# One array for the first tiles, norms by token, an earlier compression and moved tile sizes in a two-layer hybrid decoder

## The chip, the cores and the metric

The kernel runs on one core of one Trainium2 chip. The metric is the device time of the whole program in microseconds (us), from three runs: 1609.97, 1611.32 and 1611.22, median 1611.22. TensorE (PE) does the matmuls, ScalarE (ACT) and VectorE (DVE) convert and post-process, GpSimd (POOL) multiplies some tiles, and SyncE (SP) issues most of the DMAs.

## The reference

Two layers work on x of 256 tokens by 2048 features in float32. Each layer does

```python
h = rmsnorm(x, norm_w)
proj = einsum("bsd,dp->bsp", h, w_in)
(q, kc, vc, ks, vs, kw, vw, gate, z_attn, xbc, dt, z_ssm) = split_columns(proj)
k_cmp = rope(compress_blocks(kc, pe_k, w1_k, w2_k), pos_cmp)
v_cmp = compress_blocks(vc, pe_v, w1_v, w2_v)
y_attn = rmsnorm(nsa_attention(...) * silu(z_attn), norm_attn_w)
y_ssm = grouped_rmsnorm((ssd(silu(conv(xbc)), dt) + d_skip * xs) * silu(z_ssm), norm_ssm_w)
x = x + einsum("bsm,md->bsd", concat([y_attn, y_ssm]), w_out)
```

and a last rmsnorm with `final_norm_w` follows the second layer. The compression turns overlapping blocks of 32 keys (and values) into 15 compressed ones through two small matrices w1 and w2; the attention has a compressed, a selected and a windowed branch.

## The kernel before

Weights come as tiles of 128 x 1024 float32 (512 KB). SP loads them in the order of use into five raw buffers `wr` (`pump_dma`, line 147); a load is issued when DVE has used up the oldest one. Float32 accuracy is had from two reduced-precision parts: ACT copies the tile to `wh` (high part, line 122) and DVE subtracts it, `wl` = `wr` - `wh` (line 125). Both are issued by `split` (line 154), two tiles ahead of PE. The same is done to h: a tile `h` holds the high and the low part of 256 tokens each.

The work is a list (`items`, line 55). A projection item takes half of the 16 k-tiles of one tile of 128 output columns: 16 matmuls, eight of 512 moving columns with `wh` and eight of 256 with `wl`. One such item is called a slot. The first four column tiles (NF) do all their first halves (slots 0 to 3), then all their second halves (slots 4 to 7); later ones do the two halves in turn. The accumulators of later column tiles share two buffers, "pj". After the column tiles come the output projection's items in two halves ("o", 64 slots).

Post-processing is written as generators that are listed in `sides` and are moved on one step per slot by `tick` (line 327); WAITS counts the slots that each step waits. The evacuation of a finished column tile is put into `pending` and is done by `flush` in the following slot, ahead of that slot's `split`.

Around the change:

- **The head.** `FIRST` (line 92): weight 0 comes in three pieces on ACT's queue. x^T comes by `load_x` (line 185) on SP's queue, in five pieces between the first weight tiles, then `par` and `con` (lines 202, 203). Position numbers come on POOL's queue (line 384). Six matmuls on a zero tile stand before slot 0 (line 365) and eight more inside it (`WARM`, line 964).
- **The norm of layer 1** is applied to the projection's results, by a tile `rr` that holds one factor per token. ACT squares x^T in four pieces of 1024 columns, DVE adds them up in five steps (`first_slots`, line 389), PE sums over partitions with four matmuls (`rms`, line 280) at slot 5, ACT and DVE take the root at slots 6 and 7. Layer 2 has sums of squares by token from the end of layer 1 (`part`) and uses `spread_norm` (line 309) at slots 0, 1 and 2: small steps by token, then two matmuls that spread the factor over the partitions. x by token (`xT`) is loaded in slots 20 to 26 of layer 1.
- **The compression.** W1S, W1N, W1B = 9, 2, 4 (line 34): counted from the first kc tile, a group of four w-items (16 small matmuls) is put behind slot 9 and every second one after it, eight groups in all. Their moving operands are written by `build_U` (line 594) on DVE, from the evacuated kc and vc tiles. `cmp_side` (line 605) then makes the compressed keys KT and values VC, and the first `att_side` (line 688) starts when all groups are issued and the keys are there. `v_side` (line 659) transposes value tiles on PE (line 665) into a PSUM tile "t" of two buffers and copies them out on ACT and DVE as V. `gd_side` waits for rr and makes the gates.
- **The last phase.** In the second half of the output projection, `add` (line 991) adds a finished tile of 128 x 512 to `xT`, squares it on ACT and, in the last layer, multiplies it by `final_norm_w` on POOL (line 998) for the first three of four column blocks. `out_norm` (line 906) scales the rows: columns 0 to 1023 on ACT, 1024 to 1535 on DVE, the rest with the weight on DVE; all stores are issued by SP in this order.

Of the kernel before, what the change touches and what calls it, by code (L numbers as in the profile page):

```python
# [33 lines left out]
W1S, W1N, W1B = 9, 2, 4  # L34
# [53 lines left out]
def body(ctx: ExitStack, tc: tile.TileContext, wst, w1, xin, xtk, pos, w2, par, con, fin, y):  # L88
    nc = tc.nc
    ACT, DVE, PE, POOL = nc.scalar, nc.vector, nc.tensor, nc.gpsimd  # L90
    RS, RA = 5, 1
    FIRST = ((0, 256), (256, 512), (512, 1024))
# [81 lines left out]
    sqr = xt.rearrange("p a b -> p (a b)")  # L174
# [10 lines left out]
    def load_x(a, b):  # L185
        c = NK + SEQ * a if a else 0
        nc.sync.dma_start(xw[:, c:NK + SEQ * b], xin[:, c:NK + SEQ * b])

    raw[0] = sb([128, 1024], "wr", bufs=NR)
# [12 lines left out]
    nc.sync.dma_start(prm, par[0])  # L202
    nc.sync.dma_start(cst, con)
    pump_dma()
# [88 lines left out]
    part = sb([128, 2, 4], "part")  # L293

    def norm(tb, r):
        b = sb([128, 4], "nrm", bufs=2)
# [12 lines left out]
    def spread_norm(dst):  # L309
        r = sb([128, 2], "rt2")  # L310
        gens = [norm(tb, r[:, tb:tb + 1]) for tb in range(2)]
        for g in gens:
            next(g)
        for g in gens:
            for _ in g:
                pass
        yield
        ps = pst("b2", (128, 1024))
        for tb in range(2):
            mm(ps[:, 128 * tb:128 * tb + 128], r[:, tb:tb + 1].to_broadcast([128, 128]), ident, True, True)  # L320
        yield
        act(dst, ps[:, 0:256])
# [42 lines left out]
    for _ in range(6):  # L365
        mm(pz, wz[:, 0:128], wz, True, True)
# [3 lines left out]
    def make_h(a, b):  # L370
        for k in range(a, b):
            h[k] = sb([128, 512], f"h{k}", F32R)
            scaled(attn[:, k], nw0[:, k:k + 1], h[k])
# [4 lines left out]
    for j, (a, b) in enumerate(FIRST):  # L378
        make_h((0, 1, 2)[j], (1, 2, 4)[j])
        act(hi_t[0][:, a:b], raw[0][:, a:b])  # L380
        lo(lo_t[0][:, a:b], raw[0][:, a:b], hi_t[0][:, a:b])
# [4 lines left out]
    def square(c):  # L386
        act(sqr[:, c:c + 1024], reg[:, c:c + 1024], AF.Square)

    def first_slots(slot):
        if slot < 2:  # L390
            make_h(8 + 4 * slot, 12 + 4 * slot)
            square(1024 * slot)
        elif slot == 2:
            square(2048)
            tt(sqr[:, 0:1024], sqr[:, 0:1024], sqr[:, 1024:2048], OP.add)
        elif slot == 3:
            square(3072)
            tt(sqr[:, 0:1024], sqr[:, 0:1024], sqr[:, 2048:3072], OP.add)
        elif slot == 4:
            tt(sqr[:, 0:1024], sqr[:, 0:1024], sqr[:, 3072:4096], OP.add)  # L400
            tt(sqr[:, 0:512], sqr[:, 0:512], sqr[:, 512:1024], OP.add)

    sqs = [sqr[:, 0:256], sqr[:, 256:512]]

    for L in range(DEPTH):
# [500 lines left out]
        def out_norm(tb):  # L906
            r = sb([128, 1], f"rt{tb}")
            g = norm(tb, r)
            for _ in g:
                pass  # L910
            for c in range(4):
                a = xt[:, tb, 512 * c:512 * c + 512]
                if c == 3:
                    stt(a, a, r, fnw[:, 512 * c:512 * c + 512], OP.mult, OP.mult)
                elif c == 2:
                    DVE.tensor_scalar(a, a, r, None, op0=OP.mult)
                else:
                    act(a, a, scale=r)
                if c in (1, 2, 3):
                    b = 0 if c == 1 else 512 * c  # L920
                    nc.sync.dma_start(y[:, tb, b:512 * c + 512], xt[:, tb, b:512 * c + 512])
# [8 lines left out]
        for it in ITEMS:  # L930
# [21 lines left out]
            if it[0] == "p":  # L952
# [6 lines left out]
                for a in range(0, 8, n):  # L959
                    for k in range(a, a + n):  # L960
                        mm(ps, wh[:, k], src[k], first and k == 0, False)
                    for k in range(a, a + n):
                        mm(ps[:, 0:256], wl[:, k], src[k][:, 0:256], False, last and k == 7)
                    if L == 0 and slot == 0:
                        for _ in range(WARM[a]):
                            mm(pz, wz[:, 0:128], wz, True, True)
                flush()
                split(i)
            else:
# [52 lines left out]

                last4 = L + 1 == DEPTH and half and cb == 3 and kp > 3
# [13 lines left out]
                else:  # L1037
# [6 lines left out]
                    if kp == 7:  # L1044
                        add(1)
                        if half and L + 1 < DEPTH:
                            sides.append(turn())
# [13 lines left out]
            if slot == (0 if L else RS):  # L1061
                next(rgen)
            if slot == (1 if L else RS + RA):
                next(rgen)
            if slot == (2 if L else RS + RA + 1):
                for _ in rgen:
                    pass
                rr.append(rt_)
# [80 lines left out]

def layout(x, positions, norm_w, w_in, cmp_pe_k, cmp_w1_k, cmp_w2_k, cmp_pe_v, cmp_w1_v, cmp_w2_v,  # L1150
           conv_w, conv_b, dt_bias, a_log, d_skip, norm_attn_w, norm_ssm_w, w_out, final_norm_w):
    A = lambda v: np.asarray(v)
    return [
        pack_weights(A(w_in), A(w_out)),
        pack_w1(A(cmp_w1_k), A(cmp_w1_v)),
        np.ascontiguousarray(np.concatenate([
            cols(A(norm_w)[0]), A(x)[0].T.reshape(NK, 128, SEQ).transpose(1, 0, 2).reshape(128, NK * SEQ)], 1)),
# [26 lines left out]
```

## Time and profile before

| what | value |
|---|---|
| time, median of three runs | 1611.22 us |
| time of the profiled execution | 1612.35 us |
| its span | 1610.6 us |
| PE busy | 1582.5 us (98%), 9042 matmuls |
| weight loads of PE | 1353.0 us (84%), beside the matmuls |
| DVE busy | 1219.2 us (76%) |
| ACT busy | 1056.3 us (66%) |
| POOL busy | 383.9 us (24%) |
| HBM read | 298.20 MB, 186 GB/s over the span |

Busy times are those of one profiled execution, on an axis that starts with its span. A busy PE is not PE at its peak: the granted clock of a stretch is a second number to be read beside it, as tenths or hundredths of 2.4 GHz. A line such as L125 is that of a helper, so tiles say more than lines. The waits name the instruction that released the engine last.

### The profile page before, as it was taken

To read this page: it belongs to the slowest core of one execution; us is meant where nothing else is said; L and a number is where in the kernel's file an instruction comes from. 1 tells how busy PE (TensorE), PEld (TensorE's weight loads), DVE (VectorE), ACT (ScalarE), POOL (GpSimd) and SP (SyncE) were. 2 spreads that over 40 slices of the span, in tenths; PEclk is the share of its full clock that TensorE was granted. 3 is DMA by queue.
4 is the path that set the end of the run, shared out by engine and by line. 5 is a ranking of instruction groups with operands and counts; after the bars stand their busy time and mean duration, and the time that the engine had idled before them with its cause. 6 is when DMAs were issued, how large, how long until landed. Compare 5 with 4: busy or idle time off the path is not lost.

```text
span 1610.6 us, 24881 instructions
## 1 busy us (share of the span) xinstructions
PE 1582.5 (98%) x9042; PEld 1353.0 (84%) x9042; DVE 1219.2 (76%) x2113; ACT 1056.3 (66%) x1918; POOL 383.9 (24%) x314
## 2 busy tenths in 40 slices
PE   8999999999899999999999999999998999999997
PEld 7888888878788888888888888888787888888876
DVE  6888988887688786674578888888867878766654
ACT  6587777754687787544456777777447778865443
POOL 1233433431123231100012333333301323210010
PEclk9999999999999999999999999999999999999999
DMA  7575566677444444565646666666863454455653
GB/s 267 187 253 189 191 205 209 206 248 256 130 157 134 156 151 153 195 192 166 207 158 197 201 206 192 190 200 222 273 224 121 142 158 145 157 169 171 235 177 110
DMA packets 101994, 301.98 MB, mean 188 GB/s; under 512 B 9952, under 2 KB 26912, under 8 KB 101744
## 3 DMA queue, kind: packets, MB, share of 16 engines
q1 hardware_dynamic: 101024, 297.99, 56.4%
q0 software_dynamic: 416, 1.88, 0.4%
q8 instruction: 71, 1.16, 0.3%
q10 hardware_dynamic: 432, 0.52, 0.1%
q14 instruction: 51, 0.42, 0.1%
HBM read 298.20 MB, written 2.16 MB: 186 GB/s over the span
## 4 chain that ended last, share of the span: by engine, by line
PE 93%; DVE 2%; ACT 2%; DMA 1%; issue 1%; POOL 0%; ACTq 0%; SPq 0%; DVEq 0%; POOLq 0%
PE ppj L137 77%; PE po L137 7%; PE pb L137 6%; DVE wl L125 1%; ACT wh L122 1%; PE pt L137 1%; DMA wr<-wst 1%; PE pt L523 0%; PE pt L766 0%; PE po L773 0%; PE pt L767 0%; DMA V<-w 0%; DVE xT L125 0%; ACT A L122 0%; DVE A L128 0%
## 5 line engine op out<-in xcount | busy, mean ns | idle before, releaser
L125 DVE TENSOR_TENSOR wl<-wr,wh 128x1024 fp32r<-128x1024 f32 (+1 forms) x502 | 642.6, 1285 | 218.4 <-ACT wh L122 217.5
L122 ACT ACTIVATE wh<-wr 128x1024 fp32r<-128x1024 f32 (+1 forms) x502 | 517.8, 1048 | 85.6 <-PE ppj L137 46.2
L137 PE MATMUL ppj<-h,wh 128*128 128x512 f32 x1456 | 464.6, 400 | 3.1 <-DVE h L128 3.1
L137 PE MATMUL ppj<-s,wh 128*128 128x512 f32 x1456 | 462.7, 399 | 0.0
L137 PEld LDWEIGHTS ppj<-h,wl 128*128 128x128 f32 x1456 | 274.9, 189 | 65.1
L137 PEld LDWEIGHTS ppj<-s,wl 128*128 128x128 f32 x1456 | 274.4, 188 | 65.1
L137 PE MATMUL ppj<-h,wl 128*128 128x256 f32 x1456 | 288.3, 279 | 0.0
L137 PE MATMUL ppj<-s,wl 128*128 128x256 f32 x1456 | 287.3, 279 | 0.0
L340 POOL TENSOR_TENSOR uu<-uu,rr 128x256 f32<-128x256 f32 x120 | 147.7, 1232 | 525.3 <-DVE uu L125 524.0
L137 PEld LDWEIGHTS ppj<-h,wh 128*128 128x128 f32 x1456 | 223.4, 190 | 9.5 <-issue 3.3
L137 PEld LDWEIGHTS ppj<-s,wh 128*128 128x128 f32 x1456 | 222.8, 189 | 5.0 <-issue 2.7
L122 ACT ACTIVATE ev<-ppj 128x256 f32<-128x256 f32 x182 | 68.7, 378 | 210.7 <-PE ppj L137 193.7
L137 PE MATMUL ppj<-wh,h 128*128 128x512 f32 x384 | 120.4, 391 | 0.0
L137 PE MATMUL ppj<-wh,s 128*128 128x512 f32 x384 | 120.1, 391 | 0.0
L340 POOL TENSOR_TENSOR za<-za,rr 128x256 f32<-128x256 f32 x34 | 39.6, 1165 | 274.6 <-DVE za L125 239.2
L137 PEld LDWEIGHTS ppj<-wh,h 128*128 128x128 f32 x384 | 72.1, 188 | 15.6 <-DVE xT L125 0.7
L137 PEld LDWEIGHTS ppj<-wh,s 128*128 128x128 f32 x384 | 72.1, 188 | 15.5 <-DVE xT L125 0.7
L125 DVE TENSOR_TENSOR uu<-ppj,ev 128x256 f32<-128x256 f32 x116 | 48.7, 420 | 47.1 <-ACT ev L122 46.9
L122 ACT ACTIVATE A<-A,nm 128x128 f32<-128x128 f32 (+2 forms) x192 | 75.4, 394 | 7.8 <-DVE nm L716 7.6
L137 PE MATMUL ppj<-wl,s 128*128 128x512 f32 x192 | 74.9, 390 | 0.8 <-DVE wl L125 0.8
L137 PE MATMUL ppj<-wl,h 128*128 128x512 f32 x192 | 74.8, 389 | 0.0
L128 DVE SCALAR_TENSOR_TENSOR att<-uu,par,att 128x255 f32<-128x255 f32 (+2 forms) x96 | 60.5, 630 | 2.3
(244 smaller groups left out, 1980.9 us busy)
## 6 DMA issues: line engine op xcount, KB each, us to landing
wr<-wst SPq DMA_DIRECT2D x499, 512.0 KB, 3.5
V<-w SPq DMA_DIRECT2D x64, 256.0 KB, 4.8
B<-cum SPq DMA_DIRECT2D x16, 512.0 KB, 4.6
B<-cum SPq DMA_DIRECT2D x16, 256.0 KB, 5.7
xT<-xtk SPq DMA_DIRECT2D x4, 512.0 KB, 6.8
att<-xin SPq DMA_DIRECT2D x3, 512.0 KB, 8.5
att<-fin POOLq DMA_DIRECT2D x1, 1024.0 KB, 8.9
y<-xT SPq DMA_DIRECT2D x2, 512.0 KB, 2.7
```

The costliest lines, as they stand in the source:

```text
L122: ACT.activation(out, in_, f, **kw)
L125: DVE.tensor_tensor(out, a, b, op=op)
L128: DVE.scalar_tensor_tensor(out, a, s, b, op0=op0, op1=op1)
L137: PE.matmul(out, lhsT, rhs, start=start, stop=stop, skip_group_check=True)
L340: POOL.tensor_tensor(dst, dst, rr[0], op=OP.mult)
```

## The change

1. **Head.** A new array holds x tile k and slice k of weight 0 side by side for the first eight k, after the norm weights (`pack_head`). It comes in four loads on SP's queue (`HEAD`: 205, 393, 590 and 393 KB), and nothing comes on ACT's queue. Weights 1 and 2, x tiles 8 to 11, weight 3, x tiles 12 to 15 (into a tile "B"), weight 4, the first half of x by token (1 MB) and weight 5 follow in this order; weight 6 and the second half of x by token come behind the first `split`. `con` is loaded in slot 0, `par` and the positions in slot 3, all on SP. h of tiles 8 to 15 is made in slots 1 and 2 (before: 0 and 1). `WARM` gives six matmuls inside slot 0 (eight) and five stand before it (six). Weight 1 is converted in two pieces of 512.
2. **Norms.** Layer 1 uses `spread_norm` too, at slots 5, 6 and 7, from two squares of 2048 columns of x by token on ACT in slots 4 and 5. The four squares of x^T, DVE's five adds and the four matmuls of `rms` there go. Layer 2's steps are at slots 1, 3 and 4.
3. **Compression** from slot 8 (`W1S`), so each of its eight groups stands one slot earlier, and with it `cmp_side` and the condition of the first `att_side`.
4. **Order in the first 24 slots:** `split` stands ahead of `flush`.
5. **Last phase.** The multiplication by `final_norm_w` goes from POOL to DVE, two and four slots later (`weigh`). `out_norm` does columns 1024 to 1535 first and stores them, then ACT's half, stored from ACT's queue, then the last quarter.
6. **Sizes.** `con` has 848 columns (835), `part` 8 per token block (4); small tiles rt0, rt1 and rt2 go. Tiles behind `con` then start at multiples of 64 bytes.

```diff
-C_ID, C_MK, C_M2, C_CM, C_RV, C_I4, C_IF, C_SG, NC_ = 0, 128, 512, 768, 800, 801, 833, 834, 835
+C_ID, C_MK, C_M2, C_CM, C_RV, C_I4, C_IF, C_SG, NC_ = 0, 128, 512, 768, 800, 801, 833, 834, 848
-WARM = (1, 2, 1, 1, 1, 1, 1, 0)
+WARM = (2, 1, 0, 1, 1, 0, 1, 0)
-W1S, W1N, W1B = 9, 2, 4
+W1S, W1N, W1B = 8, 2, 4
-    RS, RA = 5, 1
-    FIRST = ((0, 256), (256, 512), (512, 1024))
+    HEAD = ((0, 1), (1, 3), (3, 6), (6, 8))
+    RS = ((5, 6, 7), (1, 3, 4))
...
+    NX = NK + 8 * 384
+    head = xw[:, NK:NX].rearrange("p (k c) -> p k c", k=8)
+    raw0 = head[:, :, 256:384]
+    xb = sb([128, 1536], "B", bufs=2)[:, 0:1024].rearrange("p (k c) -> p k c", k=4)
...
-    for a, b in FIRST:
-        nc.scalar.dma_start(raw[0][:, a:b], wst[0][:, a:b])
-    load_x(0, 1)
-    load_x(1, 4)
-    load_x(4, 8)
+    for a, b in HEAD:
+        c = NK + 384 * a if a else 0
+        nc.sync.dma_start(xw[:, c:NK + 384 * b], xin[:, c:NK + 384 * b])
     pump_one()
     pump_one()
-    load_x(8, 12)
+    nc.sync.dma_start(xw[:, NX:NX + 1024], xin[:, NX:NX + 1024])
     pump_one()
-    load_x(12, 16)
+    nc.sync.dma_start(xb, xin[:, NX + 1024:NX + 2048].rearrange("p (k c) -> p k c", k=4))
     pump_one()
-    nc.sync.dma_start(prm, par[0])
-    nc.sync.dma_start(cst, con)
-    pump_dma()
+    nc.sync.dma_start(xt[:, 0], xtk[:, 0])
+    pump_one()
...
-    for j, (a, b) in enumerate(FIRST):
-        make_h((0, 1, 2)[j], (1, 2, 4)[j])
...
-    make_h(4, 8)
-    split(1 - LH)
-    nc.gpsimd.dma_start(posi, bass.AP(tensor=pos.tensor, offset=pos.offset, ap=[[0, 128], [1, SEQ]]))
+    for a, b in HEAD:
+        make_h(a, b)
+        act(w0h[:, a:b], raw0[:, a:b])
+        lo(w0l[:, a:b], raw0[:, a:b], w0h[:, a:b])
+    split(1 - LH, 512)
+    nc.sync.dma_start(xt[:, 1], xtk[:, 1])
...
     def first_slots(slot):
...
+        if slot == 0:
+            nc.sync.dma_start(cst, con)
         elif slot == 3:
+            nc.sync.dma_start(prm, par[0])
+            nc.sync.dma_start(posi, bass.AP(tensor=pos.tensor, offset=pos.offset, ap=[[0, 128], [1, SEQ]]))
+        elif slot in (1, 2):
+            make_h(4 + 4 * slot, 8 + 4 * slot)
+        elif slot in (4, 5):
+            act(reg[:, 0:DM], xt[:, slot - 4], AF.Square, accum_out=part[:, slot - 4, 3:4])
...
+            q = [xt[:, tb, 512 * c:512 * c + 512] for c in range(4)]
+            DVE.tensor_scalar(q[2], q[2], r, None, op0=OP.mult)
+            nc.sync.dma_start(y[:, tb, 1024:1536], q[2])
+            for c in range(2):
+                act(q[c], q[c], scale=r)
+            nc.scalar.dma_start(y[:, tb, 0:1024], xt[:, tb, 0:1024])
+            stt(q[3], q[3], r, fnw[:, 1536:2048], OP.mult, OP.mult)
+            nc.sync.dma_start(y[:, tb, 1536:2048], q[3])
...
+                if i < 24:
+                    split(i)
                 flush()
                 split(i)
...
-                        if L + 1 == DEPTH and cb < 3:
-                            POOL.tensor_tensor(a, a, fnw[:, 512 * cb:512 * cb + 512], op=OP.mult)
...
+                def weigh(cb=cb):
+                    for tb in range(2):
+                        yield
+                        yield
+                        a = x4[:, tb, cb]
+                        tt(a, a, fnw[:, 512 * cb:512 * cb + 512], OP.mult)
...
-                rgen = spread_norm(rt_) if L else rms(sqs, DM, rt_, sb([128, 256], "uu", bufs=3))
+                rgen = spread_norm(rt_)
...
-                if slot >= 20 and slot < 28 and slot % 2 == 0:
-                    c = (slot - 20) // 2
-                    nc.sync.dma_start(xt[:, :, 512 * c:512 * c + 512], xtk[:, :, 512 * c:512 * c + 512])
...
+            if slot in RS[L]:
+                next(rgen, None)
+                if slot == RS[L][2]:
+                    rr.append(rt_)
...
+def pack_head(norm_w, x, wst):
+    xk = x[0].T.reshape(NK, 128, SEQ).transpose(1, 0, 2)
+    first = np.concatenate([xk[:, 0:8], wst[0].reshape(128, 8, 128)], 2).reshape(128, 8 * 384)
+    return np.ascontiguousarray(np.concatenate([cols(norm_w[0]), first, xk[:, 8:].reshape(128, 2048)], 1))
```

## Rows read from the trace of the kernel before

**Rows 1.** Page, busy time by engine, and the chain's shares by engine

```profile
PE 1582.5 (98%) x9042; PEld 1353.0 (84%) x9042; DVE 1219.2 (76%) x2113; ACT 1056.3 (66%) x1918; POOL 383.9 (24%) x314
...
PE 93%; DVE 2%; ACT 2%; DMA 1%; issue 1%; POOL 0%; ACTq 0%; SPq 0%; DVEq 0%; POOLq 0%
```

**Rows 2.** Waits of PE: tile, line <- releaser: us, times, longest us

```profile
PE pt L665 <- DVE V L125: 8.7, 2, 4.4
PE ppj L137 <- DVE h L128: 3.1, 2, 2.1
PE po L137 <- DVE wl L125: 1.6, 2, 0.8
...
PE pb L137 <- DVE rt L128: 1.1, 2, 0.9
PE pt L137 <- DVE att L128: 1.1, 1, 1.1
```

**Rows 3.** Half-clock windows: us; PE, PEld, DVE, ACT, POOL; PEclk; DMA share; GB/s

```profile
12.01:15.42 3.41, 3.41 (x10) 2.83 (x11) 3.14 (x5) 3.41 (x7) 0.00 (x0) 0.50 1.03 414
422.33:425.02 2.69, 2.69 (x9) 2.30 (x10) 2.32 (x10) 0.34 (x1) 0.00 (x0) 0.50 0.15 20
1215.55:1220.33 4.78, 4.78 (x16) 4.10 (x17) 4.21 (x17) 0.34 (x1) 0.00 (x0) 0.50 0.37 113
```

**Rows 4.** DMA issues, first 40 us: tiles, queue, KB, us to landing

```profile
wr<-wst ACTq DMA_DIRECT2D x1, 256.0 KB, 8.4
```

**Rows 5.** ACT, timeline 0 to 20: start us, us, instruction, idle before

```profile
4.24 0.51 ACT L122 ACTIVATE h<-att 128x256 fp32r<-128x256 f32 x1 [0.81 <-DMA att<-xin]
...
10.08 0.63 ACT L122 ACTIVATE wh<-wr 128x512 fp32r<-128x512 f32 x1 [2.92 <-DMA wr<-wst]
...
15.70 1.04 ACT L122 ACTIVATE xT<-att 128x1024 f32<-128x1024 f32 x1
```

**Rows 6.** Chain of waits, 12 to 22: start us, us, what

```profile
15.79 2.80 PE po L137 x16
```

**Rows 7.** ACT, timeline of the tail

```profile
1602.71 0.29 ACT L122 ACTIVATE nrm<-part,nrm 128x1 f32<-128x1 f32 x1
...
1603.86 1.33 ACT L122 ACTIVATE xT<-xT,rt 128x512 f32<-128x512 f32 x2 [0.61 <-DVE rt L128]
```

**Rows 8.** DVE, timeline 22 to 38

```profile
23.50 1.22 DVE L125 TENSOR_TENSOR wl<-wr,wh 128x1024 fp32r<-128x1024 f32 x1
24.64 1.22 DVE L125 TENSOR_TENSOR xT<-xT 128x1024 f32<-128x1024 f32 x1
...
36.85 0.42 DVE L128 SCALAR_TENSOR_TENSOR rr<-rr,uu 128x256 f32<-128x256 f32 x1
```

**Rows 9.** ACT, timeline around the first wait for V

```profile
414.12 0.38 ACT L122 ACTIVATE ev<-ppj 128x256 f32<-128x256 f32 x1 [5.53 <-PE ppj L137]
...
415.47 1.28 ACT L118 ACT_TABLE_LOAD   x1
...
419.12 2.20 ACT L122 ACTIVATE VC<-pt 32x128 fp32r<-32x128 f32 x8
421.34 0.38 ACT L122 ACTIVATE V<-pt 128x256 fp32r<-128x256 f32 x1
```

**Rows 10.** DVE, timeline 330 to 337

```profile
334.52 1.10 DVE L125 TENSOR_TENSOR B<-uu,par 128x256 f32<-128x256 f32 x2
```

**Rows 11.** PE, timeline 333 to 336

```profile
334.12 0.63 PE L137 MATMUL ppj<-h,wh 128*128 128x512 f32 x2
```

**Rows 12.** DVE, timeline of the last phase

```profile
1579.38 1.47 DVE L125 TENSOR_TENSOR wl<-wr,wh 128x1024 fp32r<-128x1024 f32 x1 [1.74 <-ACT wh L122]
1580.77 0.67 DVE L125 TENSOR_TENSOR xT<-xT,ppj 128x512 f32<-128x512 f32 x1
```

**Rows 13.** POOL, timeline of the last phase

```profile
1578.48 1.29 POOL L998 TENSOR_TENSOR xT<-xT,att 128x512 f32<-128x512 f32 x1 [17.73 <-ACT za L122]
```

**Rows 14.** SP, timeline of the tail

```profile
1605.22 1.63 SPq L921 DMA_DIRECT2D y<-xT  x3
```

More of the change, by code (lines that the diff above doesn't have):

```diff
@@ L183, in pump_one @@
         state["dma"] += 1
[L185 to L189, printed above, removed]
-    state["dma"] = 1
-    for a, b in FIRST:
-        nc.scalar.dma_start(raw[0][:, a:b], wst[0][:, a:b])
-    load_x(0, 1)
-    load_x(1, 4)
-    load_x(4, 8)
+    NX = NK + 8 * 384
+    head = xw[:, NK:NX].rearrange("p (k c) -> p k c", k=8)
+    raw0 = head[:, :, 256:384]
+    xb = sb([128, 1536], "B", bufs=2)[:, 0:1024].rearrange("p (k c) -> p k c", k=4)
+    xk = ([head[:, k, 0:256] for k in range(8)]
+          + [xw[:, NX + SEQ * k:NX + SEQ * k + SEQ] for k in range(4)] + [xb[:, k] for k in range(4)])
+    raw[0] = None
+    state["dma"] = 1
+    for a, b in HEAD:
+        c = NK + 384 * a if a else 0
+        nc.sync.dma_start(xw[:, c:NK + 384 * b], xin[:, c:NK + 384 * b])
     pump_one()
     pump_one()
-    load_x(8, 12)
+    nc.sync.dma_start(xw[:, NX:NX + 1024], xin[:, NX:NX + 1024])
     pump_one()
-    load_x(12, 16)
+    nc.sync.dma_start(xb, xin[:, NX + 1024:NX + 2048].rearrange("p (k c) -> p k c", k=4))
     pump_one()
-    nc.sync.dma_start(prm, par[0])
-    nc.sync.dma_start(cst, con)
-    pump_dma()
+    nc.sync.dma_start(xt[:, 0], xtk[:, 0])
+    pump_one()
     ident = cst[:, C_ID:C_ID + 128]
@@ L291, in rms, with norm @@
         stt(v, v, 1.5, y0, OP.add, OP.mult)
-    part = sb([128, 2, 4], "part")
-    def norm(tb, r):
-        b = sb([128, 4], "nrm", bufs=2)
+    part = sb([128, 2, 8], "part")
+    POOL.memset(part, 0.0)
+    def norm(tb, b):
+        r = b[:, 3:4]
         tt(b[:, 0:1], part[:, tb, 0:1], part[:, tb, 1:2], OP.add)
@@ L309, in spread_norm @@
     def spread_norm(dst):
-        r = sb([128, 2], "rt2")
-        gens = [norm(tb, r[:, tb:tb + 1]) for tb in range(2)]
+        b = [sb([128, 4], "nrm", bufs=2) for _ in range(2)]
+        gens = [norm(tb, b[tb]) for tb in range(2)]
         for g in gens:
@@ L364, in body @@
     pz = pst("b2", (128, 1024))[:, 0:512]
-    for _ in range(6):
+    for _ in range(5):
         mm(pz, wz[:, 0:128], wz, True, True)
@@ L377, in body @@
     lo_t[0] = sb([128, 1024], "wl", F32R, bufs=NL)
-    for j, (a, b) in enumerate(FIRST):
-        make_h((0, 1, 2)[j], (1, 2, 4)[j])
-        act(hi_t[0][:, a:b], raw[0][:, a:b])
-        lo(lo_t[0][:, a:b], raw[0][:, a:b], hi_t[0][:, a:b])
-    make_h(4, 8)
-    split(1 - LH)
-    nc.gpsimd.dma_start(posi, bass.AP(tensor=pos.tensor, offset=pos.offset, ap=[[0, 128], [1, SEQ]]))
-    def square(c):
-        act(sqr[:, c:c + 1024], reg[:, c:c + 1024], AF.Square)
-    def first_slots(slot):
[L390 to L395, printed above, removed]
-        elif slot == 3:
[L397 to L403, printed above, removed]
+    w0h, w0l = (t[0].rearrange("p (k c) -> p k c", k=8) for t in (hi_t, lo_t))
+    for a, b in HEAD:
[4 more added lines that the diff above has]
+    nc.sync.dma_start(xt[:, 1], xtk[:, 1])
+    def first_slots(slot):
+        if slot == 0:
+            nc.sync.dma_start(cst, con)
+        elif slot == 3:
+            nc.sync.dma_start(prm, par[0])
[4 more added lines that the diff above has]
+            act(reg[:, 0:DM], xt[:, slot - 4], AF.Square, accum_out=part[:, slot - 4, 3:4])
     for L in range(DEPTH):
@@ L906, in out_norm @@
         def out_norm(tb):
-            r = sb([128, 1], f"rt{tb}")
-            g = norm(tb, r)
+            b = sb([128, 4], "nrm", bufs=2)
+            r = b[:, 3:4]
+            g = norm(tb, b)
             for _ in g:
                 pass
[L911 to L921, printed above, removed]
+            q = [xt[:, tb, 512 * c:512 * c + 512] for c in range(4)]
[6 more added lines that the diff above has]
+            nc.sync.dma_start(y[:, tb, 1536:2048], q[3])
         def flush():
@@ L1045, in body @@
                         add(1)
-                        if half and L + 1 < DEPTH:
-                            sides.append(turn())
+                        if half:
+                            sides.append(turn() if L + 1 < DEPTH else weigh())
                 if L + 1 == DEPTH and half and cb == 0 and kp == 1:
@@ L1054, in body @@
                 rt_ = sb([128, 256], "rr")
-                rgen = spread_norm(rt_) if L else rms(sqs, DM, rt_, sb([128, 256], "uu", bufs=3))
+                rgen = spread_norm(rt_)
             if L == 0:
                 first_slots(slot)
-                if slot >= 20 and slot < 28 and slot % 2 == 0:
-                    c = (slot - 20) // 2
-                    nc.sync.dma_start(xt[:, :, 512 * c:512 * c + 512], xtk[:, :, 512 * c:512 * c + 512])
[L1061 to L1068, printed above, removed]
+            if slot in RS[L]:
+                next(rgen, None)
+                if slot == RS[L][2]:
+                    rr.append(rt_)
             tick()
```

11 lines of the change are left out of this document (5 added, 6 removed).

## The prediction

> **What bounds the kernel now.** I read the page first: PE is busy 98% of the 1610.6 us span and carries 93% of the chain that ended last [rows 1]. A change can therefore gain only where PE stands still, where it runs at half clock, or after its last matmul. The second view is PE's waits, which name five such places [rows 2]: the transposes of line 665 waited twice for V, 4.4 us at the longest; the first slots waited 2.1 us for h; the norm broadcast pb waited 1.1 us for rt; the gate transposes 1.1 us for att; and two slots of the last phase (a third is listed under another accumulator) 0.8 us each for wl. The third view is the granted clock [rows 3]: 0.50, which is 1.2 GHz, for 3.41 us in the first slot, for 2.69 us right behind the first V wait and for 4.78 us right behind the second; elsewhere it is at 2.4 GHz. PE had been idle 2.1 us and twice 4.4 us shortly before these stretches. Half clock costs half the stretch: 1.7, 1.35 and 2.39 us.
>
> The profiled execution took 1612.35 us, 1.75 us more than its span and 1.1 us above the median of 1611.22. The sum is made against it and then shifted by 1.1 us.
>
> **Head (one array, loads by date).** Today the third piece of weight 0 comes over ACT's queue and takes 8.4 us to land [rows 4]; ACT idles 2.92 us for it and converts it at 10.08 [rows 5], slot 0 crawls at half clock, and slot 1 starts at 15.79 [rows 6]. After the change the first load is 205 KB and is the first that SP issues. I take 4.2 us for its landing, as ACT's first h today starts at 4.24 [rows 5] behind a smaller load that SP issues first; the other pieces of 393, 590 and 393 KB follow at about 410 GB/s (414 in the window at 12.01 [rows 3]), at 5.2, 6.6 and 7.5. ACT then does eight h tiles (0.42 each back to back; a single one is 0.51 [rows 5]) and four weight pieces and ends near 9.6, DVE near 10.3, PE ends slot 0 at 11.2 with full clock, 12.5 with half: 3.3 to 4.6 us earlier.
> Not all of it is kept. The norm of layer 1 now needs x by token, 2 MB behind six weight tiles and all of x: 7.87 MB up to its second half, which at 414 GB/s from about 3.9 lands near 22.9. Its Square of 2048 columns (twice the 1.04 us of a 1024 one [rows 5]) ends near 27.3. The last norm of the kernel takes 1.15 us from its Ln at 1602.71 to the first use of its result at 1603.86 [rows 7]; for two halves one behind the other in part I take 1.9, so the norm's matmul at slot 6 can start at 29.2, where PE arrives at 28.0 to 29.2. I put PE behind that matmul at 29.7, against 33.4 today (slot 1 at 15.79, six slots of 2.8 [rows 6], the norm's four matmuls): **−3.7**, bounds −2.0 (the 2 MB costs more) and −5.5 (no hinge, full clock). ACT's four squares, DVE's five adds and PE's four fp32 matmuls go away; in [rows 8] a DVE operation of 1024 columns is 1.22 us. They lay beside PE, so only the time at which rr is ready matters: 37.27 today (row at 36.85 [rows 8]), 31.5 after, where slot 7 ends at 32.5. gd_side is no longer late: **−1.1** of the att wait [rows 2], bounds 0 and −1.1. POOL's position load goes to SP's queue, 128 KB behind the weights: 0.3 us of transfer at 414 GB/s, hidden by five raw buffers; without them 0.3 late.
>
> **Layer 2's norm.** Steps at slots 1, 3, 4 instead of 0, 1, 2 give Ln, Exp and three DVE steps two slots (5.6 us) instead of one before the broadcast. The waits pb <- rt go: **−1.1** [rows 2], bounds 0 and −1.1. Who uses rr is four slots later still in the queue of POOL, not of PE.
>
> **Compression a slot earlier.** Before the V wait ACT has idled 5.53 us, evacuates at 414.12, and then does in one run a table load (1.28), the softmax pieces, VC (2.20) and only then V [rows 9]. With the compression's groups at slot 8, cmp_side and the first att_side come a slot (2.79 us) earlier, v_side does not: the table load, the softmax pieces and VC move into the idle 5.53, V comes behind at most one conversion. Of each 4.36 I leave 0.7: −7.3. If the long idle goes, so do the half-clock stretches behind it: −1.35 −2.39 = −3.7.
> The other side: the first group of w-items now stands behind slot 8, and its right operand is what build_U writes. For the last kc tile DVE writes it from 334.52 to 335.62 [rows 10], while PE ends that slot near 334.2, the next slot's first pair of matmuls standing at 334.12 [rows 11]. Nothing is between any more: PE waits about 1.4 us, in both layers (the pattern of layer 2 is the same): +2.8. Sum **−8.2**; bounds −12.4 (no rest, no new wait) and +2.8 (V as late as today, new wait added).
>
> **Conversion before evacuation in the first 24 slots.** The queues of ACT and DVE take the next tile's split ahead of the evacuation. PE's accumulators have two buffers and slots come in pairs, so an evacuation may be two slots, 5.6 us, late; split costs 1.05 on ACT and 1.22 on DVE. Cost 0; with the cover gone 1.22 per slot (a rival below).
>
> **Last phase.** In three slots wl is late, and near them it takes 1.47 us [rows 12] instead of 1.22 [rows 8] where POOL's 1.29 us multiply [rows 13] runs beside it. The Trainium skill, SBUF — State Buffer, section Who interferes with whom, says that VectorE's two-input operation and a GpSimd one lock a shared port pair, the later one waiting for the earlier to end; by it wl would have ended 1.22 us after POOL's end at 1579.77, at 1580.99, and the trace has 1580.85. By this rule six such wl would give back 2.3 us (0.39 each), by the row 1.5 (0.25 each). The multiply now goes to DVE, 0.67 us as the add on the same tile [rows 12], two and four slots behind. Two such wl per gap give 0.5 us of its 0.8 back; in return 6 x 0.67 of DVE come between conversions. DVE has 1.74 us free before such a wl [rows 12], so most of it is cover: **−1.5**, bounds −2.4 (all three gaps) and +4.0 (all six multiplies on the path).
>
> **Tail.** Today the two ACT multiplies end at 1605.2 [rows 7] and the first of the last stores is issued at 1605.22, the third 0.9 us later [rows 14], because SP is in program order behind ACT's halves. In the new order DVE's q2 is stored at about 1604.45, q3 at 1605.1 and ACT's half from its own queue at 1605.2: last landing 1608.1 instead of 1609.2: **−1.1**, bounds 0 and −1.3.
>
> **Multiples of 64 bytes.** The converted tiles wr start off such a multiple today, the adds on xT start on one, and both take 1.22 us (the wl at 23.50 and the add at 24.64 [rows 8]): 0.
>
> **Sum.** −3.7 −1.1 −1.1 −8.2 −1.5 −1.1 = −16.7: 1595.65 by the profiled execution, 1594.5 by the median. All best bounds together give −23.8 (1587.4), all worst +4.8 (1616.0).
>
> **Rivals.**
> 1. *The collision stays.* The softmax pieces, VC and V still come in one run on ACT, because the first att_side is held by something else, k_side's nk say, not by w1v. For it: the run begins with a table load, which only follows from a switch of function; against it: 5.53 us of idle ahead. Compression is then worth +2.8 instead of −8.2: −5.7, 1605.5.
> 2. *Late weights.* The 2 MB of x by token stand ahead of weights 5 and 7 and take 5.1 us at 410 GB/s. If raw tiles run out around slot 4, the head's −3.7 and gd_side's −1.1 go back: −11.9, 1599.3. For it: the transfers run at 414 GB/s without a break at 12 to 15 us [rows 3]; against: 2.79 us per slot against 1.28 us per weight tile.
> 3. *The evacuation becomes the bound: slower.* If conversion ahead of evacuation delays the release of an accumulator to past two slots, PE waits a DVE subtract of 1.22 us in each of 24 slots: +29, less 16.7 elsewhere: 1624. It decides once an evacuation starts over 5.6 us after its last matmul; the one at 414.12 started as soon as PE released it [rows 9], and a conversion of about a microsecond ahead of it leaves most of a slot, so this is unlikely.
> 4. *It doesn't do what it says:* the loads land as late as now and compression only trades its wait, so the head gives 0, gd_side 0 and compression +2.8. With −1.1 −1.5 −1.1 this is −0.9: 1610.3.
>
> **How the numbers follow.** Forecast 0.64, rival 1 0.14, rival 2 0.13, rival 3 0.04, rival 4 0.05. The predicted time is the forecast's, 1594.5. The range goes from 1588 (nearly all best bounds) to 1606, which takes in rivals 1 and 2 at 1605.5 and 1599.3 and leaves out rivals 3 and 4 and part of the spread of the unknown costs. What a measurement of this kernel can tell from no change is about 0.2%, 3.2 us: forecast, rival 1 and rival 2 are faster (0.91), rival 4 is no change (0.05), rival 3 slower (0.04).
>
> **What the profile after would show.** Right: slot 1's first matmul (po) by 12.5 instead of 15.79; no PE wait for att near 64; PE waits for V under 1 us and no clock of 0.50 behind them; a new wait of about 1.4 us of the compression's matmuls for DVE's B; no wl above 1.3 us beside POOL in the last phase; last store landing 7 us behind PE's end, 1 us earlier than today. Wrong: V waits of 4 us still there (rival 1); PE waits for ACT's wh or a weight's landing in slots 4 to 8 (rival 2); matmuls waiting for an accumulator's release by DVE or ACT in the first 24 slots (rival 3).

## The result and the profile after

The changed kernel took 1594.23 us (median of four runs, 1593.54 to 1596.61) against 1611.27 us for the kernel before on the same chip; the ratio is 0.9897 with a 95% interval of 0.988 to 0.9914. The prediction was 1594.5 us, in a range of 1588 to 1606. The profiled execution took 1593.89 us with a span of 1592.1 us, 18.5 us shorter than the span of before.

The page of the kernel after, busy time by engine and the chain's shares:

```profile
PE 1575.5 (99%) x9039; PEld 1346.9 (85%) x9039; DVE 1215.1 (76%) x2128; ACT 1057.4 (66%) x1922; POOL 375.7 (24%) x308
...
PE 93%; ACT 2%; DVE 2%; DMA 1%; issue 1%; SPq 0%; DVEq 0%; ACTq 0%
```

PE is busy 7.0 us less than in [rows 1], although the 7488 weight matmuls are the same: most of that part of the 18.5 us was slow work (half clock, and small matmuls of the compression that stood and waited inside their groups), the rest was waiting and the tail. PE's waits of the kernel after (engine, tile, line <- releaser: us in total, times, longest us):

```profile
PE pt L656 <- DVE V L125: 2.5, 4, 1.1
PE pb L137 <- DVE B L125: 1.7, 2, 0.9
...
PE pb L137 <- PE ppj L137: 0.8, 1, 0.8
PE ppj L137 <- DVE h L128: 0.5, 1, 0.5
...
PE po L137 <- DVE wl L125: 0.2, 1, 0.2
```

Against [rows 2]: the two waits for V of 4.4 us are now 1.1 us, with two of 0.2 us beside them; the waits for att and rt are gone, those for wl are down to 0.2, that for h to 0.5. A wait for B is new, and so is one of 0.8 us ahead of the norm's matmuls. The windows that follow the two waits for V, of the same length as in [rows 3]:

```profile
414.59:417.28 2.69, 2.69 (x16) 2.38 (x17) 2.59 (x7) 0.91 (x6) 0.00 (x0) 1.00 0.57 181
1201.75:1206.53 4.78, 4.78 (x28) 4.22 (x29) 4.35 (x11) 2.25 (x8) 0.20 (x1) 1.00 0.57 194
```

The granted clock is 1.00 (2.4 GHz), and the windows hold 16 and 28 matmuls instead of 9 and 16: the idle times of 1.1 us were not followed by half clock here, those of 4.4 us were.

Both traces hold the same 7488 weight matmuls in the same order, so the start of one and the same matmul can be compared. The last column is what each stretch gave.

| stretch ends at | before | after | shift | of this stretch |
|---|---|---|---|---|
| slot 1, first matmul | 15.63 | 11.89 | −3.74 | −3.7 |
| slot 7, first matmul | 33.23 | 30.45 | −2.78 | +1.0 |
| behind the gate transposes | 66.13 | 62.28 | −3.85 | −1.1 |
| behind the compression, layer 1 | 454.87 | 445.90 | −8.97 | −5.1 |
| output projection, layer 1, first half | 708.46 | 701.27 | −7.19 | +1.8 |
| behind layer 2's norm | 821.94 | 813.10 | −8.84 | −1.65 |
| before the compression, layer 2 | 1111.30 | 1100.19 | −11.12 | −2.3 |
| behind it | 1249.06 | 1232.87 | −16.19 | −5.1 |
| attention, layer 2 | 1414.93 | 1397.47 | −17.46 | −1.3 |
| before the last phase's first wait for wl | 1534.31 | 1517.35 | −16.95 | +0.5 |
| last matmul | 1600.81 | 1583.48 | −17.33 | −0.4 |
| end of the span | 1610.6 | 1592.1 | −18.5 | −1.2 |

Four of these rows were not in the prediction: +1.8, −2.3, −1.3 and +0.5, stretches in which hardly anything waits in either kernel and the shift still drifts evenly. The experiments on start addresses below are about them.

### The profile page after: what moved, and what is told of

It is laid out like the page before. It is cut to its first block, busy times and chain, and to the rows that moved or that the text cites. A ratio compares the mean times of both kernels' runs of the same rounds, so it can differ in the third digit from the quotient of the medians.

```text
span 1592.1 us, 24872 instructions
## 1 busy us (share of the span) xinstructions
PE 1575.5 (99%) x9039; PEld 1346.9 (85%) x9039; DVE 1215.1 (76%) x2128; ACT 1057.4 (66%) x1922; POOL 375.7 (24%) x308
## 4 chain that ended last, share of the span: by engine, by line
PE 93%; ACT 2%; DVE 2%; DMA 1%; issue 1%; SPq 0%; DVEq 0%; ACTq 0%
PE ppj L137 77%; PE po L137 7%; PE pb L137 6%; ACT wh L122 1%; DVE wl L125 1%; DMA wr<-wst 1%; PE pt L137 0%; PE pt L758 0%; PE po L764 0%; PE pt L757 0%; PE pt L514 0%; DVE xT L125 0%; DMA att<-xin 0%; ACT A L122 0%; ACT VC L122 0%
## 5 line engine op out<-in xcount | busy, mean ns | idle before, releaser
L137 PE MATMUL ppj<-s,wh 128*128 128x512 f32 x1456 | 456.2, 395 | 0.0
```

The costliest lines, as they stand in the source:

```text
L137: PE.matmul(out, lhsT, rhs, start=start, stop=stop, skip_group_check=True)
```

## The experiments

**The date of the compression, undone in the kernel after (u_w1s).**

```diff
-W1S, W1N, W1B = 8, 2, 4
+W1S, W1N, W1B = 9, 2, 4
```

> The changed kernel with the compression put back to slot 9 (W1S = 9), nothing else. Theory 1 (as forecast: the earlier compression removes two collisions of about 3.3 us, 3.7 us of half clock behind them, and adds two waits of 0.85 us for build_U): waits of 4.4 us for V with half clock behind them are back, the waits for B are gone, and the time is 8 to 10 us longer, 1602 to 1604. Theory 2 (other parts of the change, above all the order of split and flush or the new dates of the norms, had already parted V from the softmax work): the waits for V stay near 1 us and the time is 1592 to 1595.

Measured: 1604.13 us (1603.11 to 1604.37), ratio to before 0.9949 (0.9932 to 0.9965). That is 7.5 us under the 1611.66 us of before beside it, where the kernel after was 17.0 under its own: 9.5 us of the change's 17 are lost. PE's waits have the old row back, to the tenth:

```profile
PE pt L656 <- DVE V L125: 8.7, 2, 4.4
```

and there is no row for B. The same edit alone on the kernel before **(b_w1s8)**:

> The kernel before with the compression from slot 8 (W1S = 8) and nothing else of the change. Theory 1 (the date of the compression alone parts V from the softmax work on ACT): the two waits of 4.4 us shrink to 1.1 and the half clock behind them goes, two waits for B of 0.8 to 0.9 us come; 10 us less, 1601 to 1602. Theory 2 (it needs the other parts of the change, norms or order, to have room on ACT): less than half of that, 1606 to 1611.

Measured: 1601.79 us (1601.50 to 1602.43), ratio 0.9939 (0.9922 to 0.9955), 10.3 us less than the 1612.11 us of before beside it. In the traces the last matmul starts 10.6 us earlier, but 1.2 us of this lie ahead of slot 7, where the edit changes nothing; from there on it gained 9.4 us. Its waits:

```profile
PE pt L665 <- DVE V L125: 2.8, 4, 1.1
...
PE pb L137 <- DVE B L125: 1.8, 2, 0.9
...
PE pb L137 <- DVE rt L128: 1.1, 2, 0.9
PE pt L137 <- DVE att L128: 1.1, 1, 1.1
```

The waits for rt and att are those of before, the ones for V and B those of after. The date of the compression thus does its part by itself, and needs no help from the rest of the change. Why it works can be read from ACT in the kernel after, around the first wait for V (timeline: start us, us, instruction):

```profile
404.11 1.28 ACT L118 ACT_TABLE_LOAD   x1
...
407.76 2.21 ACT L122 ACTIVATE VC<-pt 32x128 fp32r<-32x128 f32 x8
409.99 0.38 ACT L122 ACTIVATE ev<-ppj 128x256 f32<-128x256 f32 x1
...
411.22 0.38 ACT L122 ACTIVATE V<-pt 128x256 fp32r<-128x256 f32 x1
```

In [rows 9] V's copy came right behind VC, as the last piece of one run. Now that run ends before the evacuation, and V stands behind one conversion, as the prediction had it. What is left, 1.1 us each, is on DVE: V's subtraction runs from 414.03, behind six pieces of the attention's work that wait for the same slot.

**POOL's multiply, put back (u_pool).**

```diff
+                        if L + 1 == DEPTH and cb < 3:
+                            POOL.tensor_tensor(a, a, fnw[:, 512 * cb:512 * cb + 512], op=OP.mult)
...
-                        if half:
-                            sides.append(turn() if L + 1 < DEPTH else weigh())
+                        if half and L + 1 < DEPTH:
+                            sides.append(turn())
```

> The changed kernel with the multiplication by final_norm_w back on POOL and no weigh steps on DVE. Theory 1 (as forecast: VectorE's conversion is slower beside POOL's multiply): the three waits of 0.8 us of the output projection for wl are back, 1.8 us more, wl at 1.47 us beside the multiply and no other change. Theory 2 (the waits went because the first parts of the change moved the transfers): no wait over 0.3 us, same time.

Measured: one execution, 1595.5 us, which says little; the trace says it. DVE and PE's waits:

```profile
1516.61 1.48 DVE L125 TENSOR_TENSOR wl<-wr,wh 128x1024 fp32r<-128x1024 f32 x1 [1.80 <-ACT wh L122]
```

```profile
PE po L137 <- DVE wl L125: 1.3, 2, 0.7
PE ppj L137 <- DVE wl L125: 0.6, 1, 0.6
```

The slow conversions and the three waits are back. Matmul by matmul, three steps of 0.5 to 0.64 us at 1521, 1544 and 1567 us make 1.55 us.

**The order of split and flush, undone (u_order).**

```diff
-                if i < 24:
-                    split(i)
                 flush()
                 split(i)
```

> The changed kernel without the split ahead of flush in the first 24 slots. Theory 1 (as forecast, the order costs and gains nothing): the trace of the first 24 slots shifts by less than 0.5 us, time 1593 to 1596. Theory 2 (the order gave part of the head's gain, as the conversion no longer stands behind an evacuation that waits for TensorE): waits of TensorE for wh or wl appear in the first slots and the time is 1 to 3 us longer.

Measured: one execution, 1593.45 us. From the end of slot 0 on nearly all matmuls start 0.4 to 0.7 us earlier than with the new order, and no wait of more than 0.2 us comes or goes. The whole difference arises in slot 0: slot 1 starts at 11.24 instead of 11.89. Kernels that keep the new order started it between 11.26 (best_a) and 12.26 us (e_off), so the sign is not shown; the order gained nothing that can be seen here.

**The sizes alone, on the kernel before (a_sizes).**

```diff
-C_ID, C_MK, C_M2, C_CM, C_RV, C_I4, C_IF, C_SG, NC_ = 0, 128, 512, 768, 800, 801, 833, 834, 835
+C_ID, C_MK, C_M2, C_CM, C_RV, C_I4, C_IF, C_SG, NC_ = 0, 128, 512, 768, 800, 801, 833, 834, 848
-    part = sb([128, 2, 4], "part")
+    part = sb([128, 2, 8], "part")
-            r = sb([128, 1], f"rt{tb}")
+            r = part[:, tb, 4:5]
```

> The kernel before with the new sizes alone (con of 848 columns, part of 8 per block; the two small tiles rt0 and rt1 lie in part). Stationary wh and wl and the tiles h then start 384 bytes behind a multiple of 512, as after the change, the tiles s 128 behind it (192 after the change, 64 before). Theory 1 (start addresses set TensorE's pace): a 512-column matmul of the output projection takes 231 to 235 ns instead of 227, 3 to 4 us more in all, and the slots of layer 2 are faster or not by what 128 bytes make of them, 0 to -4 us; time 1610 to 1615. Theory 2 (as forecast: the sizes change nothing): every group of matmuls within 0.3% of before, 1611.3.

Measured: 1610.63 us, ratio 0.9992 (0.9982 to 1.0001). Theory 1 fell as it was put: wh did move from 320 to 384 bytes behind a multiple of 512, and the output projection's groups kept their time. Of the kernels before, a_sizes and after, the group with s as stationary tile (line, form, count | busy us, mean ns | idle us), in the window of layer 1's output projection:

```profile
L137 PE MATMUL ppj<-wh,s 128*128 128x512 f32 x256 | 80.3, 391 | 0.0
```

```profile
L137 PE MATMUL ppj<-wh,s 128*128 128x512 f32 x256 | 80.4, 392 | 0.0
```

```profile
L137 PE MATMUL ppj<-wh,s 128*128 128x512 f32 x256 | 81.7, 396 | 0.0
```

What the first two have in common, and not with the third, is the difference between the two start addresses: in before and a_sizes h and s both start at wh's address modulo 256, in after s starts 64 bytes behind it. That is a new theory: the difference counts, not the address. (The addresses follow from the order and the sizes of the tiles in the kernels; no view of the trace prints them.)

**The cost by itself (bench_offsets).** The loop over 81 pairs of tiles, each tile named by its start modulo 512:

```diff
+    for w in W:
+        for m in M:
+            ps = acc()
+            for r in range(2):
+                for a in range(0, 8, 2):
+                    for k in (a, a + 1):
+                        mm(ps, wk[:, k], mk[:, k], r == 0 and k == 0, False)
+                    for k in (a, a + 1):
+                        mm(ps[:, 0:256], wk[:, k], mk[:, k, 0:256], False, r == 1 and k == 7)
```

> This kernel leaves out the whole decoder: it only runs the two patterns of matmuls of this kernel (slots of eight 512-column and eight 256-column matmuls; triples of 512-column matmuls with the two operands exchanged) for every pair of nine start addresses of the stationary and the moving tile, 0, 64, ..., 448 and 32 bytes behind a multiple of 512, with no other engine at work. In the profile after the change the slots of layer 2 take 2.768 us instead of 2.792, those of layer 1 2.79 as before, and a 512-column matmul of the output projection 231 to 235 ns instead of 227, while the tiles moved by 64 or 128 bytes. Theory 1 (the start address of an operand sets TensorE's pace): slots differ between the pairs by about 1%, 2.77 to 2.80 us, and triples by 2 to 3%, 227 to 235 ns per matmul, in a pattern of the addresses. Theory 2 (the pace comes from other engines' or the DMAs' use of the memory): all pairs take the same time within 0.2%.

Measured, with no other engine at work but for two last memsets of DVE in the first two windows. Each window holds two slots, that is 32 matmuls (the counts take in neighbours that its edges cut); stationary tile at 0, moving tile at 0, 64, 128, 192, then stationary at 64 with moving at 64 and 128. Columns: length, PE, PEld, DVE, POOL, PEclk, DMA share, GB/s:

```profile
20.72:26.29 5.57, 5.57 (x34) 4.87 (x33) 4.74 (x2) 0.00 (x0) 1.00 0.00 0
26.29:31.84 5.55, 5.55 (x34) 4.86 (x33) 0.50 (x1) 0.00 (x0) 1.00 0.01 3
31.84:37.42 5.58, 5.58 (x35) 4.88 (x33) 0.00 (x0) 0.00 (x0) 1.00 0.00 0
37.42:42.98 5.56, 5.56 (x34) 4.87 (x33) 0.00 (x0) 0.00 (x0) 1.00 0.00 0
...
76.38:81.97 5.59, 5.59 (x35) 4.88 (x34) 0.00 (x0) 0.00 (x0) 1.00 0.00 0
81.97:87.53 5.56, 5.56 (x35) 4.87 (x34) 0.00 (x0) 0.00 (x0) 1.00 0.00 0
```

The second of the two slots, and the 24 matmuls of 512 columns in the output projection's pattern, from the start times of the matmuls:

| moving minus stationary start, modulo 256 | projection slot, ns | 512-column matmul of the output projection, ns |
|---|---|---|
| 0 | 2787 | 227 |
| 64 | 2760 | 229.6 |
| 128 | 2787 | 232 |
| 192 | 2773 | 233 |

All 64 pairs of multiples of 64 fall on the slot's values within 1 ns, at whatever address they lie, and 62 of them on those of the other pattern (two at difference 64, with the stationary tile at 64, take 233). With one tile 32 bytes off, slots take mostly 2810 to 2827 ns. So theory 1 holds with the difference in the address's place.

**The difference moved in the decoder (e_off).** One line after wl's first tile:

```diff
+    sb([128, 2, 2, 3], "nm", bufs=2)
```

> The changed kernel with the two small tiles nm allocated between wl and h0, nothing else: h then starts 128 bytes (modulo 256) behind wh and s 192; in the changed kernel it is 0 and 64. Theory 1 (the difference of the start addresses of moving and stationary tile modulo 256 sets the pace, by the table measured without the decoder): slots of layer 1 stay at 2.787 us, slots of layer 2 go from 2.760 to 2.773 (+2.4 us over 182 slots), 512-column matmuls of the output projection with h as stationary go from 227 to 232 ns (+3.9 us over 768), with s from 233 to 229.6 (-2.8 us over 768): +3.5 us in all, 1597 to 1598. Theory 2 (the start address of each tile alone counts; wh stays where it was): the output projection keeps 227 and 233 ns, and only slots may change; within 1 us of 1594.2.

Measured: 1597.99 us (1596.79 to 1599.32), ratio to before 0.9911 (0.9894 to 0.9927); the span is 1595.3 us, 3.2 above that of the kernel after. A slot of layer 2 in the chains of waits of before, after and e_off (start us, us, what):

```profile
819.08 2.79 PE pb L137 x16
```

```profile
807.07 2.76 PE ppj L137 x16
```

```profile
816.15 2.77 PE po L137 x16
```

The medians over the slots of h and of s that are followed at once by another slot are 2787 and 2787 ns in before and a_sizes, 2787 and 2760 in after, 2787 and 2774 in e_off: each where the table puts it. The output projection of e_off, first s, then h as stationary tile, and h in the kernel after:

```profile
L137 PE MATMUL ppj<-wh,s 128*128 128x512 f32 x256 | 80.8, 393 | 0.0
...
L137 PE MATMUL ppj<-wh,h 128*128 128x512 f32 x128 | 40.8, 396 | 0.0
```

```profile
L137 PE MATMUL ppj<-wh,h 128*128 128x512 f32 x128 | 40.0, 390 | 0.0
```

wh did not move here, and the matmuls with s became faster (81.7 to 80.8 us) and those with h slower (396 ns against 390 in after). The totals alone would not decide, as the intervals of the two ratios overlap; the pace of the matmuls does, and theory 2 is out.

**The grouping of 512 and 256 columns (bench_order).**

```diff
-                for a in range(0, 8, 2):
+                for a in range(0, 8, n):
```

> The decoder is left out again: only projection slots (eight matmuls of 512 columns, eight of 256), with the moving tile 0, 64, 128 or 192 bytes (modulo 256) behind the stationary one, and with groups of 1, 2, 4 or 8 k-tiles between the change from 512 to 256 columns; this kernel uses groups of 2. The first measurement of offsets gave 2787, 2760, 2787 and 2773 ns per slot for groups of 2. Theory 1 (a bank of memory that the moving stream and the loading of weights meet in): the same order of the offsets in every grouping, and groups of 2 or 1 the fastest, since eight loads of weights of 190 ns in a row do not hide behind eight matmuls of 256 columns (107 ns each at 2.4 GHz). Theory 2 (a fixed cost of changing the number of columns): the larger the group, the faster, 2.73 us or less at 8.

Measured, slots at differences 0, 64, 128 and 192: 2827, 2827, 2809, 2826 ns with groups of 1; 2787, 2760, 2787, 2775 with 2; 2807, 2771, 2809, 2775 with 4; 2793, 2770, 2811, 2778 with 8 (mean of the last three of four slots). Each difference was run with two pairs of tiles; they agree within 5 ns but for difference 0 in groups of 1, where the second pair gave 2773, so there the difference alone does not set the pace. Groups of 2 are the best or as good as any, as in the kernel; theory 2 is out. Theory 1 held in part: the order of the offsets (64, 192, 0, 128) is the same in groups of 2, 4 and 8, not in groups of 1, and but for that one pair groups of 1 are not among the fastest.

**The waits that are left (e_gaps).**

```diff
-WAITS = [1, 0, 0, 4, 0, 2, 0, 0, 0, 2, 0, 2, 0, 0, 0, 1, 1, 2, 0, 0, 0, 1, 1, 0, 3, 3, 2, 2, 0, 2, 1, 1, 2, 1, 0, 1, 1, 1, 1, 4, 3, 1, 1, 3, 4, 0, 1, 0, 0, 4, 4, 2, 2, 0, 1, 2, 0, 2, 2, 0, 1, 1, 1, 3]
+WAITS = [1, 0, 0, 4, 0, 2, 0, 0, 0, 2, 0, 2, 0, 0, 0, 1, 1, 2, 0, 0, 0, 1, 1, 0, 3, 3, 2, 2, 0, 2, 1, 1, 2, 1, 0, 1, 1, 1, 1, 4, 3, 1, 1, 2, 4, 0, 1, 0, 0, 4, 4, 2, 2, 0, 1, 2, 0, 2, 2, 0, 1, 1, 1, 3]
-        elif slot in (4, 5):
-            act(reg[:, 0:DM], xt[:, slot - 4], AF.Square, accum_out=part[:, slot - 4, 3:4])
+        elif slot == 4:
+            for tb in range(2):
+                act(reg[:, 0:DM], xt[:, tb], AF.Square, accum_out=part[:, tb, 3:4])
-                sides.append((k_side if kind[0] == "k" else v_side)(u, i, int(kind[1] == "w")))
+                if kind[0] == "k":
+                    sides.append(k_side(u, i, int(kind[1] == "w")))
+                else:
+                    sides.insert(0, v_side(u, i, int(kind[1] == "w")))
```

> The changed kernel with three edits at the waits that it has left: both Squares of x by token are issued in slot 4 (so the second does not stand on ACT behind the conversion of a weight tile that lands at 25.06 us), build_U waits two slots instead of three, and v_side is moved on ahead of the other steps of a slot. Theory 1 (each wait is set by the place of one instruction in ACT's or DVE's queue): the norm's matmuls start right behind slot 6 (1.0 to 1.6 us less), the waits of 0.8 and 0.9 us for B go (1.7 us), the waits of 1.1 us for V go (1.8 to 2.2 us): 4.5 to 5.5 us less, 1589 to 1590. Theory 2 (the waits are set by DMAs or by TensorE's own results, xT's landing, the first w1 tile, the scores): they stay or are followed by another of the same length, 1593 to 1595.

Measured: 1589.49 us (1588.72 to 1592.75), ratio to before 0.986 (0.9845 to 0.9874); the last matmul starts 5.1 us earlier than in the kernel after. The edit in WAITS is build_U's wait, one slot less (a 3 becomes a 2). PE's waits:

```profile
PE pb L137 <- PE ppj L137: 0.8, 1, 0.8
PE pt L137 <- DVE V L125: 0.7, 2, 0.3
```

B's wait is gone and V's is 0.3 us twice. The norm's 0.8 us stayed: there theory 2 was right. The chain of e_gaps shows what holds it now:

```profile
25.41 0.96 ACT wh L122
26.39 1.22 DVE wl L125
...
30.34 3.27 PE pb L137 x18
```

The Square no longer stands behind a late weight, but DVE's first step of the norm stands behind the conversion of that weight.

**One step further (best_a).** On e_gaps:

```diff
-    RS = ((5, 6, 7), (1, 3, 4))
+    RS = ((-1, 6, 7), (1, 3, 4))
+    sb([128, 2, 2, 3], "sm", bufs=2)
+    sb([128, 4], "nrm", bufs=2)
+                if L == 0 and slot == 5:
+                    next(rgen)
                 if i < 24:
                     split(i)
```

> The kernel of the run e_gaps (1589.5 us) with two more edits: the first step of layer 1's norm is issued ahead of the conversion of slot 5, and the small tiles sm and nrm are allocated between wl and h, so that h and s both start 192 bytes behind wh modulo 256. Theory 1: the norm's wait of 1.0 us at 29 us, which stayed in e_gaps because the norm's first step on DVE stood behind the conversion of the weight that lands late, goes; and by the table of offsets layer 1's slots take 2.773 us instead of 2.787, layer 2's 2.773 instead of 2.760, the output projection 229.6 ns per matmul instead of 227 and 233: -2.5 +2.4 +1.9 -2.8 = -1.0 us. Together 2 us less, 1587 to 1588. Theory 2: the wait is set by a landing and stays, and the tiles change nothing: 1589 to 1590.

Measured: 1586.65 us (1586.17 to 1589.41), ratio to before 0.9847 (0.9833 to 0.9862); it beats both kernels. Its chain runs on PE without a break through the norm's four matmuls:

```profile
25.30 2.77 PE ppj L137 x16
28.07 3.23 PE pb L137 x20
31.31 2.77 PE ppj L137 x16
```

The norm's step gave 1.6 us (the shift against e_gaps goes from −0.7 to −2.3 there). The tiles gave nothing by the end: slots take 2774 ns in both layers, as the table says, the shift reaches −4.9 in layer 1's output projection and is back at −2.3 at the last matmul, where the table had −1.0 more. Of this, 0.7 us are three waits for wl of 0.3 us in the last phase, where e_gaps has one of 0.2 us. In layer 1's projections the shift grew by 1.0 us instead of the table's 2.5; what else there changed its pace with the move (the attention's and the state space's matmuls) was not tried apart.

## Why the prediction was right, and where its steps were not

The total was right within 0.3 us of the median, and its cause was the one named; but that closeness is luck: errors of both signs cancelled, and single executions of the same kernel lie up to 3 us apart. The steps below are read from the two profiled executions, which lie 18.5 us apart, 1.4 more than the medians.

- **Compression: −8.2 forecast, −10.2 measured** in the table (−9.5 by undoing it; −10.3 by doing it alone, of which the trace puts 9.4 in and behind the compression). About 1 us of the 10.2 is not the compression's but the new addresses' (last point of this list). The waits for V lost 3.3 us each (7.3 together forecast, 6.5 measured, 0.4 of it back as two waits of 0.2), the half clock went as forecast (3.7). The new wait for B was sized at 1.4 us and is 0.82 and 0.89. DVE in the kernel after:

```profile
330.58 1.05 DVE L125 TENSOR_TENSOR B<-uu,par 128x256 f32<-128x256 f32 x2
```

  and PE:

```profile
331.20 1.07 PE L137 MATMUL pb<-V,B 128*32 128x256 f32 x16 [0.82 <-DVE B L125]
```

  The prediction took the end of both additions; PE started behind the first, before the second was done. The step also left out the loads of w1: two groups of before stretched to 2.3 us for them where the others take 1.0, the eight groups of layer 1 took 10.6 us, and in after 9.2: −1.4 us that no term had.
- **Head: −3.7 forecast, −2.8 measured.** The size is uncertain by about 1 us: slot 7 started at 33.23, 33.75 and 32.02 in before, a_sizes and b_w1s8, which share the old head, and at 30.25 to 30.58 in after, u_w1s, u_pool, e_off and e_gaps. Slot 1 started at 11.89, inside 11.2 to 12.5, and x's second half landed at 22.78 (22.9 forecast). The forecast read the clock as full outside the three windows of [rows 3]; but a 512-column matmul takes 0.63 us, as at half clock, up to 8.3 us in before, and in after up to 10.2 (PE's timeline):

```profile
9.38 0.63 PE L137 MATMUL pb<-za 128*128 128x512 f32 x1
...
10.38 0.39 PE L137 MATMUL pb<-za 128*128 128x512 f32 x1
```

  So slot 0 ran for the most part at half clock and ended between the two times forecast. The term that was mis-sized is the time between the landing and the norm's matmul. The chain of waits of the kernel after:

```profile
12.73 12.33 DMA wr<-wst
...
25.17 1.07 ACT wh L122
...
26.26 1.23 DVE wl L125
...
30.21 3.27 PE pb L137 x18
```

  A weight tile that SP had issued behind the 2 MB of x landed at 25.06, and its conversion stood ahead of the second Square on ACT and of the norm's first step on DVE. That Square ended at 28.39 (27.3 forecast) and the norm's second pair of matmuls started at 30.21 (29.2 forecast for the norm's matmul). The forecast's hinge was right, its time was 1 us too early. This is rival 2's transfer, but it cost 1 us and not 4.8: PE never waited for the weight itself.
- **gd_side: −1.1 forecast, −1.07 measured.** The wait for att is gone.
- **Layer 2's norm: −1.1 forecast, −1.65 measured.** The waits for rt went; the rest lies in the norm's four matmuls, which ran as two pairs of 0.49 us each, 0.72 us apart, and now run in one piece of 0.60 us.
- **Last phase: −1.5 forecast, −1.8 measured** in three steps of 0.6 us, and −1.55 by undoing it. No wl takes over 1.3 us there any more.
- **Tail: −1.1 forecast, −1.1 measured** (9.35 to 8.22 us behind PE's end). The issues come in the order and nearly at the distances forecast; in SP's timeline of after, against one run of three in [rows 14]:

```profile
1587.05 0.33 SPq L905 DMA_DIRECT2D y<-xT  x1
1587.71 0.33 SPq L910 DMA_DIRECT2D y<-xT  x1
```

- **Multiples of 64 bytes: 0 forecast, 0 to −1 measured, for a wrong reason.** The step looked at ACT's and DVE's rows and never asked whether PE minds where its operands lie. It does: the new sizes, with the new order of the tiles, made the slots of layer 2 27 ns shorter (−2.3 and −1.3 us, and about −1 inside the compression's stretch) and the matmuls of the output projection that read s 6 ns longer (+1.8 in layer 1; +0.5 and, with the 1.8 us of waits taken out of −0.4, +1.4 in the last phase). Without the compression's stretch these sum to +0.1 us. For that stretch u_w1s is the witness, with the new sizes and the old compression: between 1111 and 1249 us of before it gained 0.3 us on it, although its groups of compression matmuls took 0.8 us longer there. That gains and losses nearly cancelled is luck too: with h and s moved by another 128 bytes, in e_off, the same change ends with a span that is 3.2 us longer.

None of the rivals' signs showed: no V wait of 4 us (rival 1), no wait of PE for wh or a landing in slots 4 to 8 (rival 2), no matmul waiting for an accumulator in the first 24 slots (rival 3), and the parts did what they say (rival 4). Two of the forecast's own signs were missed in size: the V waits are 1.06 and 1.11 us and not under 1, and B's wait is not 1.4.

## What to carry to other kernels

Where an engine waits for the last piece of a long run of work on another engine, look for idle time of that other engine just ahead of the run: moving the run's first input one slot earlier gave 9 to 10 of the 17 us, the half clock behind the wait included. Where an edit moves tiles in memory, compare the spacing of PE's matmuls in a stretch without waits before and after; a drift that was even per matmul came here from the addresses and not from a queue. And look for what stands ahead of a moved step in each engine's queue, not only for when its input lands.

## What the runs showed of the hardware

In the kernel's grouping by twos, the pace of these matmuls depends on the difference of the start addresses of the moving and the stationary tile modulo 256 bytes, by 1.0% for a projection slot (2760 to 2787 ns) and 2.6% for the output projection's matmul (227 to 233 ns), and by more where one is 32 bytes off a multiple of 64 (up to 2827 ns for a slot). The two patterns want different differences, 64 and 0, and since h and s serve both, no common place won both here; weight tiles at two offsets were not tried. The Trainium skill, TensorE: Matmul & The Clock Gate, section Step-by-step: what each phase is for, says that the streaming operand and the loading of weights have read ports of their own, so that a load takes no bandwidth from a running matmul. The measurement of offsets shows that the pace of the two together is not independent of each other's addresses; what they meet in, no run here shows.
